# Convolution layers: output projection per third of the tokens, LayerNorm of the later thirds beside it

## The chip, the cores and the metric

The kernel runs on one core of a Trainium2 chip. The metric is the device time of one execution in microseconds. The core has five engines that run their own instruction queues in order: TensorE (PE, matrix multiply), VectorE (DVE), ScalarE (ACT), GpSimd (POOL) and SyncE (SP, which here only issues DMAs). Instructions of different engines wait for each other by semaphores.

## The reference, cut to what matters

A trunk of four layers works on 128 context tokens and 1024 latent tokens of width 1024. Layers 0 and 3 are widened Conformer convolution modules, layer 1 is neighbourhood attention, layer 2 is a state-space mixer. The change concerns the convolution layers:

```python
def conformer_conv_mixer(h, w_in, b_in, w_dw, b_dw, ln_w, ln_b, w_out, b_out):
    v, g, z = jnp.split(h @ w_in + b_in, 3, axis=-1)
    u = v * jax.nn.sigmoid(g)
    u = depthwise_conv(u, w_dw, b_dw)              # 31 taps along the tokens
    u = jax.nn.silu(layer_norm(u, ln_w, ln_b))     # mean and variance over the 1024 channels
    return (u * jax.nn.silu(z)) @ w_out + b_out

# each layer
h, gate = modulated_norm(x, cond, ada_w, ada_b, norm_w)   # RMSNorm(x) * (1 + scale) + shift
x = x + gate * mixer(h)
```

After the last layer a final RMSNorm follows. All is float32.

## The kernel before, in words

Channels lie on the 128 partitions, in eight tiles (KT = 8, index m or k); the 1152 tokens are the free axis, in three thirds of 384 (b = 0, 1, 2; the first holds the context and 256 latent tokens). A product in float32 is made as three products of rounded halves: activations are kept as hh + hl (or gh + gl), weights as wh + wl. A *unit* (`unit`, L471 to L473) is one weight tile of 1024 x 128 times one third: 8 x 3 = 24 matmuls into one PSUM bank.

Weights stream in a fixed order (`weight_specs`): SP loads a raw tile of 512 KB (three buffers), ACT casts it to wh (L432), and one engine named by `w_eng` subtracts to give wl (L433): POOL in the convolution layers, POOL and DVE by turns in part of layer 2. There are two buffers of wh and wl. `ahead` prepares the next one when one is taken.

The order of work is written out by hand with generators. After each unit `tick` (L480 on) pops four depthwise steps, advances the first generator in `gens` three times and runs deferred pieces. A planner then orders the instructions of each engine at build time by a simulated time line, so an instruction can stand earlier or later in its queue than its place in the text.

A convolution layer (`conv_layer`) goes over the channel tiles: the g and v units of tile m, their product u, then the depthwise convolution of that tile as steps: 21 taps on DVE (L773, L775, the sum lies in PSUM as ca) and 10 taps as a scale on ACT (L767) and a sum on POOL (L768), and an addition of both (L784) into c. Tiles of z, the third part of w_in, are put in between as `TAIL` lists them: z tile 5 and 6 come after the last v tile, z tile 7 in the tail. z goes to DRAM and is read back in pieces (zk).

The last channel tile's convolution is split by thirds. Then comes the tail. `conv_norm` of a third has these steps: one for the channel sums by matmul with ones (L648) and the mean (L716); eight that subtract the mean (L720, by turns DVE and POOL), square (ACT, L722) and add up the squares by matmul (L723); the row of variances turned into columns by tiny matmuls (L314), 1/sigma by Newton steps on DVE (L323 to L331), spread over the partitions by a diagonal (dg, L340) and a matmul (rs_ps, L344), four steps later; then eight steps that scale (L731, DVE), silu (L733, ACT), times z (L734, DVE), cast to gh (L735, ACT) and subtract to gl (L736, POOL).

Before the change the tail runs the first third's LayerNorm with four remaining convolution steps beside each of its steps, then all remaining convolution steps of both other thirds, then the rest of the first LayerNorm with the second's first nine steps beside it and z tile 7 between. The pools are closed and others opened, and the output projection (`out_proj`) begins: first a group of the thirds 0 and 1, in which each weight tile serves two units (the first two tiles are taken together), then a group of third 2. The second LayerNorm's rest and the third LayerNorm are generators that advance three steps a unit. Each unit of the projection (`out_unit`) adds the bias on ACT (L557), evicts on DVE (L566), squares on ACT and sums the squares on POOL (L296); in layer 3 it also turns the result (L1517, L1519). After a group the next layer's norm of those thirds follows.

At the start (`start`), layer 0's modulation is computed, and the input norms of the thirds 0 and 1 are written out in front of the first unit; that of third 2 is a generator.

Of the kernel before, what the change touches and what calls it, by code (L numbers as in the profile page):

```python
# [19 lines left out]
P = 128  # L20
# [19 lines left out]
TAIL0 = ([(), (), (0,), (1,), (2,), (3,), (4,), (5, 6)], (7,), 0, 10)  # L40
TAIL3 = ([(), (), (0,), (1,), (2,), (3,), (4,), (5, 6)], (7,), 1, 10)
# [33 lines left out]
REST = 4  # L75
# [5 lines left out]
VAR_MM = 2  # L81
# [93 lines left out]
class Kern:  # L175
    def __init__(self, ctx, tc, A, O, depth):
        self.tc, self.nc, self.A, self.O = tc, tc.nc, A, O
        nc = self.nc
        self.const = ctx.enter_context(tc.tile_pool(name="const", bufs=1))
        self.blkp = ctx.enter_context(tc.tile_pool(name="blk", bufs=9))  # L180
        self.wraw = ctx.enter_context(tc.tile_pool(name="wraw", bufs=3))
        self.wsp = ctx.enter_context(tc.tile_pool(name="wsp", bufs=2))
        self.work = ctx.enter_context(tc.tile_pool(name="work", bufs=2))
        self.dram = ctx.enter_context(tc.tile_pool(name="dram", bufs=1, space=DRAM))
        self.mmp = ctx.enter_context(tc.tile_pool(name="mm", bufs=3, space=PSUM))
        self.xs = [A["x"]] + [self.dram.tile([P, KT, T], F32, name=f"xs{i}") for i in range(1, DEPTH)]
        self.pend, self.steps, self.trickle, self.gens, self.slow = [], [], [], [], []
        self.raws, self.split, self.wi = {}, {}, 0
        self.w_eng = nc.gpsimd
        self.h = [None] * NB  # L190
        self.ada_end = lambda: None
        self.depth = depth
        self.specs = self.weight_specs()
# [113 lines left out]
    def rstd_row(self, row, n, eps):  # L307

        nc = self.nc
        ps = self.mm("st_ps")  # L310
        s = self.work.tile([P, BW], F32, name="row", tag="dg", bufs=1)
        nc.scalar.copy(out=s[0:1, :], in_=row[0:1, :])
        for j in range(3):
            nc.tensor.matmul(ps[:, j:j + 1], lhsT=s[0:1, j * P:(j + 1) * P], rhs=self.ones[0:1, 0:1], start=True,  # L314
                             stop=True)
        return (yield from self.spread(self.rsqrt(ps[:, 0:3], n, eps)))
# [17 lines left out]
    def spread(self, y, times=1.0):  # L334

        nc = self.nc
        for _ in range(LAG):
            yield
# [32 lines left out]
    def weight_specs(self):  # L371
# [5 lines left out]
        for l in range(self.depth):  # L377
# [29 lines left out]
            if kind != 2:  # L407
                out += [(w[m], P) for g in range(2) for m in range(KT)]
# [15 lines left out]
    def wsplit(self, i):  # L424
        if i < len(self.specs) and i not in self.split:
# [7 lines left out]
            self.w_eng.tensor_tensor(out=wl[:, :, :width], in0=s, in1=wh[:, :, :width].bitcast(F32),  # L433
# [46 lines left out]
    def tick(self):  # L480
# [4 lines left out]
        for _ in range(GENS_A_UNIT):  # L485
            self.advance()
# [89 lines left out]
    def out_proj(self, l, g, bias=None, order=None):  # L576
        nc = self.nc
        with self.tc.tile_pool(name="xm", bufs=2, reuse_waits="tile") as pool:
            self.out_begin(l, bias, pool)
            for grp in ((0, 1), (2,)):  # L580
                x0, x1 = (grp[0] * BW, (grp[-1] + 1) * BW) if order is None else (0, T)
                for ms in [(0, 1)] + [(m,) for m in range(2, KT)]:
                    w, xm = {}, {}
                    for m in ms:
                        w[m] = self.wtake()
                        xm[m] = pool.tile([P, x1 - x0], F32, name="xm", tag="xm", bufs=2)
# [17 lines left out]
    def conv_layer(self, l, j, order):  # L604
        nc, tc, h = self.nc, self.tc, self.h
        with tc.tile_pool(name="cp", bufs=1, space=PSUM, reuse_waits="tile") as cp, ExitStack() as stack:
            cw = stack.enter_context(tc.tile_pool(name="cw", bufs=2, reuse_waits="tile"))
            close = stack.close
# [78 lines left out]
            self.lz = cw  # L687
            rest = run(chain(*rest))
            lns[0] = also(lns[0], rest, REST)
            z, nz = chain(*[z_tile(m) for m in TAIL[l][1]]), NB * len(TAIL[l][1])  # L690
            interleave(part(z, TAIL[l][2]), TAIL[l][2], part(lns[0], 9), 9)
            for _ in rest:
                pass
            lns[0] = also(lns[0], part(lns[1], 9))
            interleave(part(lns[0], TAIL[l][3]), TAIL[l][3], z, nz - TAIL[l][2])
            self.flush()
            close()
            with tc.tile_pool(name="lz", bufs=3, reuse_waits="tile") as self.lz:
                for _ in lns[0]:
                    pass  # L700
                self.gens += lns[1:]
                self.out_proj(l, g, bias=("conv_b_out", j * KT), order=order)

    def conv_norm(self, cp, b, j, c, s1, sums, zd, g):

        nc = self.nc
        if b == VAR_MM:
            self.var = cp.tile([P, 3 * 512], F32, name="var", tag="ca", bufs=1)
# [9 lines left out]
        var = self.var[:, 512 * b:512 * b + BW] if b >= VAR_MM else self.mm("var")[:, :BW]  # L718
        for k in range(KT):
# [3 lines left out]
            nc.tensor.matmul(var, lhsT=self.ones, rhs=sq, start=(k == 0), stop=(k == KT - 1))  # L723
            yield
        r = yield from self.rstd_row(var, D, LN_EPS)
        gh, gl = self.blk(f"gh{b}", F32R), self.blk(f"gl{b}", F32R)
        for k in range(KT):
            z = self.lz.tile([P, BW], F32, name="zk", tag="zk", bufs=3)
# [7 lines left out]
            nc.gpsimd.tensor_tensor(out=gl[:, k, :], in0=ck, in1=gh[:, k, :].bitcast(F32), op=ALU.subtract)  # L736
# [802 lines left out]
    def start(self, pool):  # L1539
# [31 lines left out]
        for k in range(KT):  # L1571
# [15 lines left out]
        steps(1, 1 + LAG + 9)  # L1587
# [95 lines left out]
```

## Time and profile before

| | |
|---|---|
| time, median of 3 runs | 2935.44 us (2934.78 to 2937.71) |
| the profiled execution | 2928.56 us, its span 2926.8 us |
| PE busy | 2775.3 us (95%) |
| PE weight loads busy | 2522.4 us (86%) |
| DVE busy | 1976.1 us (68%) |
| ACT busy | 1415.6 us (48%) |
| POOL busy | 1262.1 us (43%) |

The shares are means over the whole span. The two tails of the convolution layers are from about 389 to 580 us and from about 2730 to 2914 us of the span, and what matters in them is read stretch by stretch. Busy time includes time in which an instruction has begun and is held up.

### The profile page before, as it was taken

Reading aid. Unit: us, or ns where it says so; the run is one execution under the profiler, and the core shown is the slowest. Engines: PE = TensorE matmul, PEld = TensorE weight load, DVE = VectorE, ACT = ScalarE, POOL = GpSimd, SP = SyncE. Lnnn points to the kernel's source line nnn. Section 1 sums busy time; section 2 is a strip of 40 time slices with the busy share of each in tenths; the row PEclk is TensorE's granted clock in tenths of the full one; section 3 lists DMA queues with packets and bytes.
Section 4 is the critical chain, followed back from the end, with each engine's and each line's share of the span. In section 5 each row is a group of like instructions: output and inputs, shape, how many; then the busy total and the mean of one; then the engine's idle time right before and its main releaser. Section 6 shows DMA issues by size and latency. Waiting matters only on the chain. (4 is left out here: it accounts for less than half of the span.)

```text
span 2926.8 us, 46350 instructions
## 1 busy us (share of the span) xinstructions
PE 2775.3 (95%) x17561; PEld 2522.4 (86%) x17561; DVE 1976.1 (68%) x3283; ACT 1415.6 (48%) x2764; POOL 1262.1 (43%) x764
## 2 busy tenths in 40 slices
PE   5999998999999999999999999999999999999888
PEld 4999977989999998888999998887778889999678
DVE  5899886553444444536787677866885565999973
ACT  4455455443333333444443336865663444555553
POOL 4688766601011101245113442312433346888765
PEclk9999999999999999999999999999999999999989
DMA  5232324632222323336235559977896752111134
GB/s 223 68 121 98 103 78 150 210 118 79 82 83 89 92 81 102 121 102 208 81 89 160 162 166 314 342 219 229 271 322 227 253 176 85 55 65 53 62 122 142
DMA packets 231551, 424.48 MB, mean 145 GB/s; under 512 B 19552, under 2 KB 149408, under 8 KB 231328
## 3 DMA queue, kind: packets, MB, share of 16 engines
q1 hardware_dynamic: 229280, 417.50, 44.1%
q10 hardware_dynamic: 2048, 4.02, 0.4%
q8 instruction: 139, 2.28, 0.3%
q14 instruction: 84, 0.69, 0.1%
HBM read 331.83 MB, written 79.66 MB: 141 GB/s over the span
## 5 line engine op out<-in xcount | busy, mean ns | idle before, releaser
L433 POOL TENSOR_TENSOR wl<-raw,wh 128x1024 fp32r<-128x1024 f32 x169 | 408.3, 2417 | 951.4 <-ACT wh L432 909.5
L775 DVE SCALAR_TENSOR_TENSOR ca<-u,vec,ca 128x1167 f32<-128x1167 f32 (+4 forms) x420 | 481.4, 1146 | 11.3
L768 POOL TENSOR_TENSOR pa<-pa,pt 128x1167 f32<-128x1167 f32 (+4 forms) x189 | 399.6, 2117 | 78.4 <-ACT pa L763 36.4
L432 ACT CAST wh<-raw 128x1024 fp32r<-128x1024 f32 (+1 forms) x239 | 249.3, 1043 | 351.0 <-PE op L472 84.9
L471 PE MATMUL in_ps<-hh,wh 128*128 128x384 f32 x768 | 268.4, 352 | 4.2 <-DVE nt L866 3.0
L472 PE MATMUL in_ps<-hl,wh 128*128 128x384 f32 x768 | 262.4, 342 | 0.7 <-DVE hl L364 0.7
L473 PE MATMUL in_ps<-hh,wl 128*128 128x384 f32 x768 | 261.9, 341 | 0.0
L767 ACT ACTIVATE pt<-u,vec 128x1167 f32<-128x1167 f32 (+4 forms) x189 | 193.9, 1039 | 128.3 <-POOL pa L768 127.2
L471 PE MATMUL op<-gh,wh 128*128 128x384 f32 x576 | 202.0, 353 | 18.2 <-ACT gh L735 12.0
L1410 ACT ACTIVATE rw<-rw,nal 128x128 f32<-128x128 f32 x576 | 175.8, 389 | 76.0 <-DMA rw<-ssd_rows 75.9
L473 PE MATMUL op<-gh,wl 128*128 128x384 f32 x576 | 199.9, 348 | 10.1 <-POOL wl L433 10.1
L1289 DVE SCALAR_TENSOR_TENSOR sca<-ub,vec,sca 128x1155 f32<-128x1155 f32 x144 | 205.0, 1424 | 3.5
L471 PE MATMUL x_ps<-hh,wh 128*128 128x384 f32 x576 | 203.9, 354 | 1.3 <-ACT ub L1240 0.7
L472 PE MATMUL op<-gl,wh 128*128 128x384 f32 x576 | 202.0, 351 | 0.5 <-POOL gl L736 0.5
L473 PE MATMUL x_ps<-hh,wl 128*128 128x384 f32 x576 | 196.5, 342 | 0.0
L472 PE MATMUL x_ps<-hl,wh 128*128 128x384 f32 x576 | 196.5, 341 | 0.0
L471 PEld LDWEIGHTS in_ps<-hh,wh 128*128 128x128 f32 x768 | 145.3, 189 | 13.8 <-issue 7.3
L296 POOL TENSOR_TENSOR ssq<-ssq,sq 128x384 f32<-128x384 f32 x105 | 111.6, 1064 | 86.5 <-ACT sq L295 85.3
L472 PEld LDWEIGHTS in_ps<-hl,wh 128*128 128x128 f32 x768 | 145.6, 190 | 3.2 <-DVE hl L364 1.5
L473 PEld LDWEIGHTS in_ps<-hh,wl 128*128 128x128 f32 x768 | 145.5, 189 | 3.1 <-issue 2.4
L471 PE MATMUL op<-sgh,wh 128*128 128x384 f32 x384 | 135.6, 353 | 5.1 <-DVE xm L566 2.6
L473 PE MATMUL op<-sgh,wl 128*128 128x384 f32 x384 | 134.4, 350 | 4.8 <-POOL wl L433 4.3
(280 smaller groups left out, 7552.4 us busy)
## 6 DMA issues: line engine op xcount, KB each, us to landing
raw<-in_ada_w SPq DMA_DIRECT2D x96, 512.0 KB, 4.5
rw<-ssd_rows SPq DMA_DIRECT2D x72, 512.0 KB, 5.9
raw<-in_ssd_w_in SPq DMA_DIRECT2D x62, 512.0 KB, 4.4
raw<-in_conv_w_in SPq DMA_DIRECT2D x48, 512.0 KB, 3.5
raw<-in_ssd_w_out SPq DMA_DIRECT2D x48, 512.0 KB, 4.6
raw<-in_conv_w_out SPq DMA_DIRECT2D x32, 512.0 KB, 3.7
raw<-in_na_w_in SPq DMA_DIRECT2D x32, 512.0 KB, 3.6
ssd_xtok<-xtk SPq DMA_DIRECT2D x20, 576.0 KB, 3.6
```

Source lines behind the costliest of these rows:

```text
L296: nc.gpsimd.tensor_tensor(out=acc, in0=acc, in1=sq, op=ALU.add)
L432: nc.scalar.copy(out=wh[:, :, :width], in_=s)
L433: self.w_eng.tensor_tensor(out=wl[:, :, :width], in0=s, in1=wh[:, :, :width].bitcast(F32), op=ALU.subtract)
L471: nc.tensor.matmul(out, lhsT=wh[:, k, :width], rhs=hh[:, k, :], start=f, stop=False)
L472: nc.tensor.matmul(out, lhsT=wh[:, k, :width], rhs=hl[:, k, :], start=False, stop=False)
L473: nc.tensor.matmul(out, lhsT=wl[:, k, :width], rhs=hh[:, k, :], start=False, stop=l)
L767: nc.scalar.activation(out=pt, in_=u_t, func=AF.Copy, scale=wt(t))
L768: nc.gpsimd.tensor_tensor(out=p, in0=p, in1=pt, op=ALU.add)
L775: nc.vector.scalar_tensor_tensor(out=c, in0=u_t, scalar=wt(t), in1=c, op0=ALU.mult, op1=ALU.add)
L1289: nc.vector.scalar_tensor_tensor(out=ca, in0=u[:, t:t + SCLEN], scalar=wt(t), in1=ca, op0=ALU.mult, op1=ALU.add)
L1410: nc.scalar.activation(out=e, in_=e, func=AF.Identity, bias=self.nal[:, c, d, 8 * g + q:8 * g + q + 1])
```

## The change

- `TAIL`: z tile 6 joins z tile 7 in the tail, in both layers.
- The remaining convolution steps of the second and the third third are kept apart. The first LayerNorm has two steps of the second third beside each of its first nine steps, with z tile 6; then z tile 7 beside the 1/sigma chain; then one such step beside each of its last steps. All that remains (the second third's last steps, the second LayerNorm, the last third's convolution one step beside each of its steps, the third LayerNorm) becomes one generator, advanced five steps a unit in the projection.
- `out_proj` in these layers goes through three groups of one third, so that each weight tile is loaded, cast and split once for each third: 24 instead of 16. Its pool is the convolution's own, which stays open; xm has the buffers of sg and zt, zk is three parts of an old u buffer.
- In that projection every third weight split is DVE's.
- `conv_norm`: the variance's bank is one of the two of the sums (for the last third that of ca); from the second third on, the variance matmul comes one step after its square, and the 1/sigma matmuls three and twelve steps later; every second gl is DVE's.
- `start`: the spread of the first norm comes one pair of modulation tiles later; the second third's norm is a generator.

```diff
-TAIL0 = ([(), (), (0,), (1,), (2,), (3,), (4,), (5, 6)], (7,), 0, 10)
-TAIL3 = ([(), (), (0,), (1,), (2,), (3,), (4,), (5, 6)], (7,), 1, 10)
+TAIL0 = [(), (), (0,), (1,), (2,), (3,), (4,), (5,)], (6, 7)
+TAIL3 = TAIL0
-REST = 4
+REST = 2, 1
+LAG_TAIL = 12
+RATE_TAIL = 5
...
-    def rstd_row(self, row, n, eps):
+    def rstd_row(self, row, n, eps, lag):
...
+        for _ in range(lag // 4 - 1):
+            yield
...
-        for _ in range(LAG):
+        for _ in range(lag):
             yield
...
+            eng = self.w_eng[i % len(self.w_eng)] if isinstance(self.w_eng, list) else self.w_eng
...
-        for _ in range(GENS_A_UNIT):
+        for _ in range(self.rate):
             self.advance()
...
+            grps = ((0,), (1,), (2,)) if pool else ((0, 1), (2,))
...
-                for ms in [(0, 1)] + [(m,) for m in range(2, KT)]:
+                for ms in [(0, 1)] + [(m,) for m in range(2, KT)] if len(grps) == 2 else [(m,) for m in range(KT)]:
...
-            self.lz = cw
-            rest = run(chain(*rest))
-            lns[0] = also(lns[0], rest, REST)
-            z, nz = chain(*[z_tile(m) for m in TAIL[l][1]]), NB * len(TAIL[l][1])
-            interleave(part(z, TAIL[l][2]), TAIL[l][2], part(lns[0], 9), 9)
-            for _ in rest:
+            self.zk = [up[KT % 3][:, i * BW:(i + 1) * BW] for i in range(3)]
+            rest = [run(r) for r in rest]
+            ln0 = also(lns[0], rest[0], REST[0])
+            z = chain(*[z_tile(m) for m in TAIL[l][1]])
+            interleave(part(ln0, 9), 9, part(z, 3), 3)
+            interleave(part(lns[0], 1 + LAG), 1 + LAG, z, 3)
+            for _ in also(lns[0], rest[0], REST[1]):
                 pass
-            lns[0] = also(lns[0], part(lns[1], 9))
-            interleave(part(lns[0], TAIL[l][3]), TAIL[l][3], z, nz - TAIL[l][2])
             self.flush()
-            close()
-            with tc.tile_pool(name="lz", bufs=3, reuse_waits="tile") as self.lz:
-                for _ in lns[0]:
-                    pass
-                self.gens += lns[1:]
-                self.out_proj(l, g, bias=("conv_b_out", j * KT), order=order)
+            self.gens += [chain(rest[0], also(lns[1], rest[1], 1), rest[1], lns[2])]
+            self.rate, self.w_eng = RATE_TAIL, [nc.gpsimd, nc.vector, nc.gpsimd]
+            self.out_proj(l, g, bias=("conv_b_out", j * KT), order=order, pool=cw)
+            self.rate, self.w_eng = GENS_A_UNIT, nc.gpsimd
...
-        var = self.var[:, 512 * b:512 * b + BW] if b >= VAR_MM else self.mm("var")[:, :BW]
+        shape, tag, bufs = ([P, 512], "s1", 2) if b < 2 else ([P, 3 * 512], "ca", 1)
+        var, todo = cp.tile(shape, F32, name="var", tag=tag, bufs=bufs)[:, :BW], []
...
-            nc.tensor.matmul(var, lhsT=self.ones, rhs=sq, start=(k == 0), stop=(k == KT - 1))
+            todo.append((k, sq))
+            if b == 0 or len(todo) == 2:
+                i, q = todo.pop(0)
+                nc.tensor.matmul(var, lhsT=self.ones, rhs=q, start=(i == 0), stop=(i == KT - 1))
             yield
-        r = yield from self.rstd_row(var, D, LN_EPS)
+        for i, q in todo:
+            nc.tensor.matmul(var, lhsT=self.ones, rhs=q, start=False, stop=True)
+        r = yield from self.rstd_row(var, D, LN_EPS, LAG_TAIL if b else LAG)
...
-            z = self.lz.tile([P, BW], F32, name="zk", tag="zk", bufs=3)
+            z = self.zk[k % 3]
...
-            nc.gpsimd.tensor_tensor(out=gl[:, k, :], in0=ck, in1=gh[:, k, :].bitcast(F32), op=ALU.subtract)
+            (nc.gpsimd if k % 2 else nc.vector).tensor_tensor(out=gl[:, k, :], in0=ck, in1=gh[:, k, :].bitcast(F32),
+                                                              op=ALU.subtract)
...
             if k == NORM_0:
-                steps(0, 1 + LAG + k)
+                steps(0, 1)
+            elif k == NORM_0 + 1:
+                steps(0, LAG + k)
...
-        steps(1, 1 + LAG + 9)
+        self.gens.append(norms[1])
```

## Rows read from the trace of the kernel before

**Rows 1.** Busy time by stretch, layer 0's tail: stretch, length, busy (instructions), clock, DMA.

```profile
398.00:441.00 43.00, 35.53 (x133) 25.09 (x134) 40.79 (x67) 22.06 (x46) 23.22 (x19) 0.88 0.17 59
441.00:480.00 39.00, 28.36 (x120) 23.82 (x120) 29.88 (x44) 21.05 (x44) 26.19 (x23) 0.87 0.49 153
...
497.00:560.00 63.00, 61.41 (x354) 60.48 (x353) 32.68 (x58) 33.92 (x63) 43.73 (x29) 1.00 0.62 210
```

**Rows 2.** The same, tail of layer 3 (PE, PEld, DVE, ACT, POOL).

```profile
2736.00:2775.00 39.00, 29.75 (x104) 19.11 (x104) 38.34 (x64) 23.66 (x46) 27.21 (x24) 0.96 0.03 8
2775.00:2801.00 26.00, 15.47 (x62) 13.46 (x62) 23.20 (x44) 12.34 (x26) 14.16 (x14) 0.71 0.43 143
...
2834.00:2914.00 80.00, 78.86 (x474) 77.35 (x473) 38.58 (x81) 38.64 (x67) 52.29 (x35) 1.00 0.41 135
```

**Rows 3.** Waits, 395 to 581 us: who waited for whom, total, times, longest.

```profile
PE rs_ps L344 <- DVE dg L340: 8.1, 3, 5.0
PE op L471 <- ACT gh L735: 8.1, 2, 6.5
...
PE op L473 <- POOL wl L433: 5.5, 4, 2.1
```

**Rows 4.** DVE's groups, 395 to 581: count, busy us, mean ns, idle before.

```profile
L734 DVE TENSOR_TENSOR c<-c,zk 128x384 f32<-128x384 f32 x24 | 22.2, 961 | 5.0 <-DMA zk<-zd 2.8 <-ACT gh L735 1.1 <-ACT sq L722 1.0
L775 DVE SCALAR_TENSOR_TENSOR ca<-u,vec,ca 128x384 f32<-128x384 f32 x32 | 19.8, 618 | 0.5
L731 DVE SCALAR_TENSOR_TENSOR c<-c,vec,rstd 128x384 f32<-128x384 f32 x24 | 17.6, 801 | 2.3 <-ACT rstd L346 2.3
L566 DVE SCALAR_TENSOR_TENSOR xr<-op,mod,nt 128x384 f32<-128x384 f32 (+2 forms) x32 | 15.5, 510 | 42.7 <-PE op L473 42.7
...
L720 DVE TENSOR_TENSOR c<-c,mu 128x384 f32<-128x384 f32 x12 | 11.2, 986 | 0.0
```

**Rows 5.** Timeline of DVE and POOL at the ends of stretches: start us, us, instructions merged.

```profile
388.24 0.62 DVE L784 TENSOR_TENSOR c<-ca,pa 128x128 f32<-128x128 f32 x2
...
450.10 1.02 DVE L734 TENSOR_TENSOR c<-c,zk 128x384 f32<-128x384 f32 x2
...
452.09 8.06 DVE L731 SCALAR_TENSOR_TENSOR c<-c,vec,rstd 128x384 f32<-128x384 f32 x8 [0.97 <-ACT rstd L346]
...
453.53 5.14 POOL L720 TENSOR_TENSOR c<-c,mu 128x384 f32<-128x384 f32 x4
...
2729.80 0.62 DVE L784 TENSOR_TENSOR c<-ca,pa 128x128 f32<-128x128 f32 x2 [0.17 <-POOL pa L768]
...
2785.98 1.36 DVE L734 TENSOR_TENSOR c<-c,zk 128x384 f32<-128x384 f32 x1
```

**Rows 6.** Timeline of PE inside a full unit.

```profile
369.68 0.33 PE L471 MATMUL z_ps<-hh,wh 128*128 128x384 f32 x1
...
370.20 0.33 PE L471 MATMUL z_ps<-hh,wh 128*128 128x384 f32 x1
```

**Rows 7.** PE's groups, 390 to 700: count, busy us, mean ns, idle.

```profile
L723 PE MATMUL var<-sq,ones 128*128 128x384 f32 x48 | 19.8, 520 | 0.0
```

**Rows 8.** Single lines over the whole span: duration ns shortest/median/longest.

```profile
L433 POOL TENSOR_TENSOR wl<-raw,wh x169: 1282/2397/3579, 35.2 to 2906.0; 128x1024 fp32r<-128x1024 f32 x168, 128x512 fp32r<-128x512 f32 x1
...
L433 DVE TENSOR_TENSOR wl<-raw,wh x70: 1200/1225/2083, 1756.4 to 2347.2; 128x1024 fp32r<-128x1024 f32 x70
...
L734 DVE TENSOR_TENSOR c<-c,zk x48: 543/1000/2470, 436.3 to 2848.8; 128x384 f32<-128x384 f32 x48
...
L736 POOL TENSOR_TENSOR gl<-c,gh x48: 995/1236/1341, 441.3 to 2854.0; 128x384 fp32r<-128x384 f32 x48
```

**Rows 9.** Waits of PE, 2350 to 2430, end of layer 2's projection.

```profile
PE op L473 <- POOL wl L433: 4.3, 3, 2.1
```

**Rows 10.** Timeline of PE, last matmul of layer 0's projection.

```profile
579.41 0.34 PE L473 MATMUL op<-gh,wl 128*128 128x384 f32 x1
```

**Rows 11.** Timeline of PE in front of the first unit.

```profile
62.72 1.62 PE L344 MATMUL rs_ps<-dg,ones 128*128 128x384 f32 x2 [7.81 <-DVE dg L340]
```

More of the change, by code (lines that the diff above doesn't have):

```diff
@@ L80 @@
 VEC0 = sum(n for _, n in VECS[:4])
-VAR_MM = 2
 NA_FIRST = (0, 1), (2,), (3,)
@@ L189, in __init__ @@
         self.w_eng = nc.gpsimd
+        self.rate = GENS_A_UNIT
         self.h = [None] * NB
@@ L315, in rstd_row @@
                              stop=True)
-        return (yield from self.spread(self.rsqrt(ps[:, 0:3], n, eps)))
+        return (yield from self.spread(self.rsqrt(ps[:, 0:3], n, eps), lag=lag))
     def rsqrt(self, x, n, eps):
@@ L332, in rsqrt, with spread @@
         return y
-    def spread(self, y, times=1.0):
+    def spread(self, y, times=1.0, lag=LAG):
         nc = self.nc
-        for _ in range(LAG):
+        for _ in range(lag):
             yield
@@ L407, in weight_specs @@
             if kind != 2:
-                out += [(w[m], P) for g in range(2) for m in range(KT)]
+                out += [(w[m], P) for g in range(NB if kind == 0 else 2) for m in range(KT)]
         return out
@@ L574, in out_unit, with out_proj @@
             nc.sync.dma_start(out=self.xs[l + 1][:, :, b * BW:(b + 1) * BW], in_=self.xb[b])
-    def out_proj(self, l, g, bias=None, order=None):
+    def out_proj(self, l, g, bias=None, order=None, pool=None):
         nc = self.nc
-        with self.tc.tile_pool(name="xm", bufs=2, reuse_waits="tile") as pool:
+        with ExitStack() as stack:
+            grps = ((0,), (1,), (2,)) if pool else ((0, 1), (2,))
+            pool = pool or stack.enter_context(self.tc.tile_pool(name="xm", bufs=2, reuse_waits="tile"))
             self.out_begin(l, bias, pool)
-            for grp in ((0, 1), (2,)):
+            for grp in grps:
                 x0, x1 = (grp[0] * BW, (grp[-1] + 1) * BW) if order is None else (0, T)
-                for ms in [(0, 1)] + [(m,) for m in range(2, KT)]:
+                for ms in [(0, 1)] + [(m,) for m in range(2, KT)] if len(grps) == 2 else [(m,) for m in range(KT)]:
                     w, xm = {}, {}
@@ L605, in conv_layer @@
         nc, tc, h = self.nc, self.tc, self.h
-        with tc.tile_pool(name="cp", bufs=1, space=PSUM, reuse_waits="tile") as cp, ExitStack() as stack:
-            cw = stack.enter_context(tc.tile_pool(name="cw", bufs=2, reuse_waits="tile"))
-            close = stack.close
+        with tc.tile_pool(name="cp", bufs=1, space=PSUM, reuse_waits="tile") as cp, \
+                tc.tile_pool(name="cw", bufs=2, reuse_waits="tile") as cw:
             up = [cw.tile([P, ULEN], F32, name=f"u{i}", bufs=1) for i in range(3)]
```

7 lines of the change are left out of this document (3 added, 4 removed).

## The prediction

> **What bounds the kernel now.** I read first the busy share of each engine in stretches of the two convolution tails, then the waits there, then VectorE's groups, then the timeline at the ends of the stretches. In the first tail PE is busy 35.5 of 43 us, then 28.4 of 39, then 61.4 of 63; in the last layer's it is 29.8 of 39 and 15.5 of 26, then 78.9 of 80 [rows 1, 2]. So PE loses time from the end of the depthwise convolution until two thirds of the tokens have passed their LayerNorm, and is full from there. In those stretches DVE is busy 40.8 of 43 and 38.3 of 39 us. What PE waits for are products of LayerNorm: the normalised gh, 8.1 us, and the row of 1/sigma (dg), 8.1 us; late weights (wl) cost 5.5 us [rows 3]. The granted clock is 0.88 and 0.87 in the two loose stretches of layer 0 and 0.71 in the loosest of layer 3, against 1.00 where PE is full [rows 1, 2]: a pause also makes the matmuls behind it slower.
>
> The timeline says why DVE is late. The first third of the last convolution tile is done at 388.9 and at 2730.4; the last multiplies by z that this third's gh waits for start at 450.1 and 2786.0 [rows 5]. These 62 and 56 us hold all taps of both other thirds (32 of L775, 19.8 us [rows 4]) and part of the second LayerNorm, and then the second third is wanted after two units of projection.
>
> **The change, part by part.** The sum is made in the profiled run's own clock: span 2926.8, the run 2928.56. The median of the runs shown is 2935.44, so 6.9 us are added at the end.
>
> Unit prices. Three matmuls of a unit start every 0.52 us [rows 6], so a unit of 24 takes 4.17 us. With what lies between, I take 4.35 in layer 0 and 4.7 in layer 3, where each unit also turns its result (17 units in the 80 us full stretch, 474 records [rows 2]). A pass of statistics (eight matmuls of the variance, or seven of the sum) is a third of the 19.8 us of row L723, less the overlap of its pairs: 5.8 us [rows 7]. DVE prices are means of the same stretch [rows 4]: subtract mean 1.0 (four a third, POOL has the other four), scale 0.73 to 0.80, times z 0.96, a tap 0.62, eviction 15.5 us for 20 units = 0.78. The 1/sigma chain counts 5.0, the longest wait of PE for it [rows 3].
>
> *First LayerNorm.* Of the second third's 32 convolution steps two now go with each of nine LayerNorm steps and one with each of eight, 26 in all, some 18 of them DVE's taps; the last third's stay behind the first gh. DVE: entry 2 (estimate), subtract 4, taps 18 x 0.62 = 11, chain 5, scale 8 x 0.8 = 6.4, times z 7.7, and the four gl that move here from POOL, 4 x 0.96 = 3.8 by the nearest two-input row: 40 us. The first gh is whole at 429 instead of 451 and at 2770.5 instead of 2787. PE meanwhile has two z tiles, 25 us, of which the moved one fills the time in which DVE still runs taps; it cost 12.5 us of PE before and costs the same now. If it were placed too late it would stand after gh, at worst 12.5 us a layer.
>
> *Second LayerNorm beside eight units.* DVE between first and second gh: three taps 2, all 21 taps of the last third 13, subtract 4, chain 5, scale 6.4, times z 7.7, gl 3.8, evictions 6.2, and one weight split in three. That split on DVE has rows from the SSD layer: 1.20 to 2.08 us, median 1.23 [rows 8]; 2.7 of them at 1.4 make 3.7. Sum 52 us; in layer 3 also eight copies of turned output (0.5 each, estimate by L566), 56. PE has after its first unit (paced by gh, done 2 us after it) seven more and a variance pass: 7 x 4.35 + 5.8 = 36 in layer 0, 7 x 4.7 + 5.8 = 39 in layer 3. So PE would wait 52 - 2 - 36 = 14 and 56 - 2 - 39 = 15 us. With the shortest times seen in place of means (times z 0.543 [rows 8]; 0.55 for subtract and gl, an estimate by it) the DVE sum falls by 4 + 2 + 2 + 1 and the wait to 5. I take 8 us: POOL loses a half of its gl here but keeps 2.39 us for each of two splits in three, so I stand between the ends.
>
> *Third LayerNorm beside eight units.* DVE 4 + 5 + 6.4 + 7.7 + 3.8 + 6.2 + 3.7 = 37; PE 36, and the sums of the last third, 5.8, that no longer come early since their bank is now shared with the variance. 42 against 37: no wait in layer 0, 45 against 41 in layer 3.
>
> *The end of each tail.* From the first finished unit (431, 2772.5) PE has 23 units and three passes of statistics: 23 x 4.35 + 17.4 = 117.5 and 23 x 4.7 + 17.4 = 125.5. Without waiting it is done at 548.5 and 2898, with 8 us at 556.5 and 2906. Now the projection ends at 579.7 [rows 10] and at 2914 [rows 2]; the 12.8 us from there to the span's end stay. Gains: 23 and 8 us.
>
> *Eight more weight tiles a layer.* A tile for each unit instead of one for two. A weight is cast on ACT and split on POOL, the split alone 2.39 us [rows 8] against 4.35 of PE, in two buffers. The last 80 us of the SSD layer's projection already run so, one weight a unit, with the next layer's norm beside them: 4.3 us of waits for wl [rows 9], in 80 / 4.7 = 17 units 0.3 us each, and that is inside the 4.35. The loads: 1.1 MB a unit at most, as in the full stretch 497 to 560, whose DMA share is 0.62 [rows 1]; I cost them at nothing. If that cover is gone, the cast waits behind SP's queue, where the z slices now wait for one of three pieces of an old buffer, as they do now for one of three tiles.
>
> *Lag of the matmuls, rate 5, the variance's bank.* Each takes a wait of PE's queue away where DVE is late; what is then late is gh itself, counted above. Zero by themselves.
>
> *The start.* The first unit stands behind a 1/sigma matmul of the second third, which waits 7.8 us for DVE until 62.7 [rows 11]. With the change that norm comes behind the first unit. Its own DVE chain ends no earlier, and the third unit hangs on it, so at most the 7.8 us come back, and if its matmul slides behind a whole unit 4.2 are lost. I take -3.
>
> Sum: -23 - 8 - 3 = -34, 2894.6 for a run like the profiled one, 2901 beside the median.
>
> **A rule weighed.** Where POOL is busy, times z takes 1.0 us in the median and up to 2.47, where 0.543 is its shortest, and POOL's gl 1.24 against 0.995 [rows 8]. In one stretch four subtracts on POOL (5.14 us) ran beside eight scales on DVE (8.06 us) [rows 5]: the 2.9 us that DVE had alone hold some five scales at 0.55 to 0.6 (estimate by times z's 0.543), so the 5.14 us hold four POOL pieces and three scales, whose short times add up to 4.0 + 1.8 = 5.8. They overlap by little. The Trainium skill, SBUF — State Buffer, section Who interferes with whom, says that a DVE instruction with two SBUF inputs and a GpSimd one that reads SBUF exclude each other, the second blocked until the first ends. The trace nearly agrees (5.14 for 5.8). By that rule the gl and splits moved to DVE stand in one line with POOL's work; what that gives is the second rival.
>
> **The rivals.**
> 1. *The waits vanish* (DVE's short times hold; chance 0.15): 548.5 and 2898, start -6: -31 - 16 - 6 = -53, 2882. For it: POOL has less to do. Against: 38.3 of 39 us DVE [rows 2].
> 2. *POOL and DVE take turns* (0.18). Beside the first eight units POOL has 5.3 splits x 2.39, 8 square sums, 8 LayerNorm pieces and 11 tap sums at 1.0 each (estimate by gl's 0.995), 40 us; DVE's two-input work is 17 us by shortest times. 57 in line; the third LayerNorm 46. PE then waits 20 us in layer 0 and 15 in layer 3: -11 - 2 - 3 = -16, 2919. For it: the 2.47 us in [rows 8] and the pair in [rows 5]. Against: the 52 us of DVE above already hold the slowed means, and only what exceeds them is new.
> 3. *The weight feed decides, slower* (0.16). Place: 32 units in two layers have a LayerNorm beside them and a weight of their own. ACT's cast stands in order behind silu and casts of gh, and holds them up when it waits for a weight buffer; the split stands behind LayerNorm on POOL. Price: the longest wait for wl is 2.1 us [rows 3, 9]. From 34 / 32 = 1.1 us a unit the gain is gone; at 2 us the time is 2935 - 34 + 64 = 2965. Against: 0.3 us a unit in [rows 9].
> 4. *The order stays* (0.06): instructions are issued in the order a planner finds at build time; if it hoists the same work as now, 2935.
>
> **How the numbers follow.** Forecast 0.45, own range 2890 to 2912. The range 2871 to 2932 takes in rivals 1, 2 and the middle of 4; left out are rival 3 beyond its point, and little below. 0.2% (5.9 us) is what a measurement can tell here. Faster: 0.45 + 0.15 + 0.18 + 0.01 = 0.79; same: 0.05 of rival 4 and 0.02 of 3 = 0.07; slower 0.14.
>
> **What would show it.** The last multiply for the first third's gh near 429 and 2770; one wait of PE for gh of 5 to 15 us after eight units and none after sixteen; projection over near 556 and 2906; L433 wl waits under 10 us a layer. Wrong: wl or wh as PE's largest waits (rival 3), times z well over 1.0 us in the mean (rival 2), or a first gh later than 440, which would say the planner put other work in front.

## The result and the profile after

| | before | after |
|---|---|---|
| median of 4 runs | 2936.24 us (2934.78 to 2937.71) | 2962.68 us (2959.22 to 2964.99) |
| span of the profiled execution | 2926.8 us | 2962.0 us |
| layer 0: last v matmul, first and last matmul of the projection | 366.1, 440.9, 579.7 | 363.3, 438.6, 598.9 |
| layer 3: the same | 2704.4, 2775.2, 2914.0 | 2721.5, 2797.6, 2948.7 |

The ratio is 1.0097, with a 95% interval of 1.0080 to 1.0114: 26 us slower, where 34 us faster was forecast. From the last v matmul to the end of the projection layer 0 now takes 235.6 us (213.6 before), layer 3 227.2 us (209.6). The profiled run of the kernel before is 7.7 us under its median and the changed one 1.1 us over: that is why the spans are 35 us apart and the medians 26.

Busy time of the changed kernel in the stretches of [rows 1] and [rows 2]; columns as there (PE, PEld, DVE, ACT, POOL, granted clock, DMA):

```profile
398.00:441.00 43.00, 30.35 (x125) 22.41 (x124) 41.42 (x72) 22.29 (x44) 20.77 (x18) 0.84 0.41 138
441.00:480.00 39.00, 37.63 (x192) 34.28 (x191) 14.08 (x31) 19.08 (x37) 19.24 (x13) 0.96 0.55 178
497.00:560.00 63.00, 52.17 (x263) 47.00 (x261) 47.95 (x82) 34.53 (x64) 30.72 (x20) 0.92 0.64 219
...
2834.00:2914.00 80.00, 64.42 (x324) 56.91 (x323) 63.88 (x98) 42.70 (x76) 48.02 (x29) 0.89 0.47 149
```

The first unit comes only 2.3 us earlier. The next stretch, loose before, is nearly full (37.6 of 39 us). But the stretches that were full are loose now: 52.2 of 63 us where it was 61.4, and 64.4 of 80 where it was 78.9, with DVE busier by 15 and 25 us (in layer 3 the work arrives some 20 us later, so that the stretch still holds a part of the LayerNorms). With the pauses the granted clock there falls from 1.00 to 0.92 and 0.89.

Waits of PE in the changed kernel, 395 to 600 us (total, times, longest), beside [rows 3]:

```profile
PE rs_ps L348 <- DVE dg L344: 18.1, 3, 9.1
PE var L729 <- ACT sq L725: 11.8, 3, 10.8
PE op L476 <- ACT gh L743: 6.3, 1, 6.3
PE op L478 <- POOL wl L438: 3.2, 2, 2.0
PE op L477 <- DVE gl L744: 2.5, 1, 2.5
```

Weights are hardly waited for (3.2 us). Two of the waits for dg, 8.1 and 9.1 us, stand in front of the next layer's norms, at 549 and 569 us; a wait of 10.8 us for the second LayerNorm's squares stands in front of the first unit. DVE at the second dg, and POOL beside it, from the changed kernel's timelines (start, us):

```profile
557.38 2.28 DVE L368 SCALAR_TENSOR_TENSOR hl<-nt,mod,hh 128x128 fp32r<-128x128 f32 x1
...
566.41 0.16 DVE L333 SCALAR_TENSOR_TENSOR nr_z<-nr_y,nr_a 128x3 f32<-128x3 f32 x1
566.61 0.96 DVE L334 TENSOR_TENSOR nr_z<-nr_z,nr_y 128x3 f32<-128x3 f32 x1
567.60 0.16 DVE L335 SCALAR_TENSOR_TENSOR nr_y<-nr_z,nr_y 128x3 f32<-128x3 f32 x1
```

```profile
557.12 2.40 POOL L438 TENSOR_TENSOR wl<-raw,wh 128x1024 fp32r<-128x1024 f32 x1 [7.79 <-ACT wh L436]
566.56 0.99 POOL L298 TENSOR_TENSOR ssq<-ssq,sq 128x384 f32<-128x384 f32 x1 [7.04 <-ACT sq L297]
```

This is the reading to learn. An instruction of 0.16 us on three columns takes 0.96 us because it began 0.05 us after a POOL instruction of 0.99 us, and ends with it. A subtraction on 128 columns takes 2.28 us beside a weight split of 2.40 us. DVE counts as busy all that time, and the wait of PE is written against dg, not against POOL. The whole stretch, 395 to 600 us of the changed kernel, says the same: the scale of 384 columns (L739) takes 0.61 us in the mean of the 13 that no POOL instruction overlaps and 1.45 us in the 11 that one does; times z (L742) takes 0.55 and 1.07; a convolution tap (L784), whose sum lies in PSUM, takes 0.62 both ways.

### The profile page after: what moved, and what is told of

It is laid out like the page before. It is cut to its first block, busy times and chain, and to the rows that moved or that the text cites. A ratio compares the mean times of both kernels' runs of the same rounds, so it can differ in the third digit from the quotient of the medians.

```text
span 2962.0 us, 46434 instructions
## 1 busy us (share of the span) xinstructions
PE 2790.2 (94%) x17561; PEld 2534.5 (86%) x17561; DVE 2007.2 (68%) x3323; ACT 1436.4 (48%) x2780; POOL 1244.7 (42%) x740
## 3 DMA queue, kind: packets, MB, share of 16 engines
q8 instruction: 139, 2.28, 0.3%
## 5 line engine op out<-in xcount | busy, mean ns | idle before, releaser
L784 DVE SCALAR_TENSOR_TENSOR ca<-u,vec,ca 128x1167 f32<-128x1167 f32 (+4 forms) x420 | 481.5, 1146 | 11.3
L436 ACT CAST wh<-raw 128x1024 fp32r<-128x1024 f32 (+1 forms) x255 | 266.4, 1045 | 375.7 <-PE op L477 94.2
L298 POOL TENSOR_TENSOR ssq<-ssq,sq 128x384 f32<-128x384 f32 x105 | 118.5, 1129 | 83.7 <-ACT sq L297 82.2
L438 DVE TENSOR_TENSOR wl<-raw,wh 128x1024 fp32r<-128x1024 f32 x86 | 112.0, 1302 | 46.2 <-ACT wh L436 45.5
```

Of the source, the lines that this page charges most:

```text
L298: nc.gpsimd.tensor_tensor(out=acc, in0=acc, in1=sq, op=ALU.add)
L436: nc.scalar.copy(out=wh[:, :, :width], in_=s)
L784: nc.vector.scalar_tensor_tensor(out=c, in0=u_t, scalar=wt(t), in1=c, op0=ALU.mult, op1=ALU.add)
```

## The experiments

Ratios are against the kernel before, run on the same chip beside each group of runs. Its median there is 2936.4 us for a to d, 2932.9 for e to h, 2933.5 for i, j, k and m, and 2932.5 for n, o and p. Two versions are compared by their medians; by the spread of the runs such a difference is good to 4 to 7 us (9 for h), and between groups it also holds up to 4 us of the chips. All edits but the last lie in the two convolution layers; m also changes a lag in the norms behind them.

**Undoing orders in the changed kernel.** Four runs: the rate back to three (a), a shorter lag (b), the first LayerNorm in front of the last taps on DVE (c), all three (d).

```diff
-            self.gens += [chain(rest[0], also(lns[1], rest[1], 1), rest[1], lns[2])]
+            self.gens += [chain(rest[0], also(lns[1], rest[1], 1), rest[1], lns[2], self.slow_down())]   # a: rate = 3
...
-LAG_TAIL = 12
+LAG_TAIL = 4                                           # b
...
+            rest[1] = self.behind(rest[1], self.last_mul)   # c: each step issued behind the first LayerNorm's last L742
```

> The rate of side work goes back from five steps a unit to three once the convolution's LayerNorms are through, so that the next layer's norms run at the old spacing. Theory 2 (at rate five the multiply that spreads a norm's 1/std stands one unit behind its row): the two PE waits for dg in layer 0 (8.1 and 9.1 us in the changed kernel) go to under 1 us each, layer 3 has no such wait, and the time falls by 13 to 17 us, to about 2947. Theories 1 and 3 (the LayerNorms' chains) and the rivals (24 weights to feed, POOL and DVE on one port) are not touched by it: by them alone it stays within 3 us of 2963.

> The lag between the later LayerNorms' statistics and the matmul that spreads 1/std is cut from 12 steps to 4. Theory 1 (the second LayerNorm is late because its short chain stands at fixed places among PE's units, with DVE idle): 1/std of layer 0 is there some 5 to 7 us earlier, the wait for the second gh (6.3 and 2.5 us for gl in layer 0, 8.5 us in layer 3) goes to under 3 us, the time falls by 8 to 15 us, to about 2951. Rival 1 (DVE's load or POOL and DVE in turns makes the second LayerNorm late): the wait stays above 5 us and the time within 3 us of 2963. Rival 2 (the lag was needed): a PE wait of 3 to 6 us for dg appears at the shortened place and eats the gain.

> DVE's queue gets the last third's taps of the last convolution tile behind the last product of the first LayerNorm, by an order written into the kernel, not left to the planner. Theory 3 (the planner's order puts 20 taps of 620 ns in front of the first LayerNorm's multiplies): the first gh is whole near 429 instead of 441 in layer 0, the first projection unit starts 9 to 12 us earlier in both layers, the time falls by 18 to 24 us, to about 2942. If the second LayerNorm or the weight feed sets the end whatever comes first, the first unit is earlier but the projection ends where it did, the wait for the second gh grows by as much, and the time stays within 5 us of 2963.

> The three edits together (rate back to three for the next layer's norms, lag 4, last taps behind the first LayerNorm's products). If the three theories hold and add up: 15 + 12 + 22 us off, about 2914, 22 us below the kernel before. If the second LayerNorm's place bounds what an earlier first gh can give: about 2935. If the weight feed of 24 weights or the port decides: above 2950.

Measured: a 2956.7 (1.0077, 1.0058 to 1.0095), b 2963.3 (1.0097, 1.0078 to 1.0116), c 2959.0 (1.0081, 1.0063 to 1.0099), d 2946.5 us (1.0043, 1.0025 to 1.0062). So a is worth 6 us, b nothing, c 4 (a and c are hardly beyond the spread), all three 16: a third of the 49 us expected, and no mending. In a, the dg wait fell to 9.0 us, but a wait of 8.2 us for an eviction came in front of the next layer. In b the wait for the second gh went (6.3 us), and the longest dg wait grew from 9.1 to 11.9. In c the first unit started at 438.9, where 429 was expected. PE's timeline of d:

```profile
420.42 0.81 PE L655 MATMUL s<-c,ones 128*128 128x384 f32 x2
431.59 1.65 PE L741 MATMUL var<-sq,ones 128*128 128x384 f32 x2 [10.36 <-ACT sq L737]
433.03 5.86 PE L655 MATMUL s<-c,ones 128*128 128x384 f32 x14
438.72 0.81 PE L741 MATMUL var<-sq,ones 128*128 128x384 f32 x2
439.07 0.81 PE L476 MATMUL op<-gh,wh 128*128 128x384 f32 x2
```

The planner puts two variance matmuls of the second LayerNorm ahead of the first unit, and PE waits there for squares that DVE's and ACT's queues hold behind the first LayerNorm. That is not all: gh itself is whole no earlier than in the changed kernel (440.4 us there, 440.4 in c, 440.9 in d). In c DVE has dg done at 415.2, but PE, which has z to do, comes to its matmul only at 419.4, and then rstd stands in ACT's queue behind a wait for xm and the cast of a weight:

```profile
419.92 0.80 ACT L562 ACTIVATE nt<-xm,gb 128x128 f32<-128x128 f32 x2 [2.05 <-DMA xm<-in_x]
420.63 1.03 ACT L436 CAST wh<-raw 128x1024 fp32r<-128x1024 f32 x1
...
422.04 0.47 ACT L350 ACTIVATE rstd<-rs_ps 128x384 f32<-128x384 f32 x1
```

So the scale of the first LayerNorm begins at 422.8 us in c and at 423.9 in the changed kernel, though 19 taps of the last third have left its way. A chain that is put right in one queue waits in the next.

**One part alone, on the kernel before.** f: the projection by thirds with 24 weight tiles. g: z tiles 6 and 7 in the tail.

```diff
-            for grp in ((0, 1), (2,)):
+            for grp in ((0,), (1,), (2,)) if bias else ((0, 1), (2,)):                        # f
-                for ms in [(0, 1)] + [(m,) for m in range(2, KT)]:
+                for ms in [(m,) for m in range(KT)] if bias else [(0, 1)] + [(m,) for m in range(2, KT)]:
...
-TAIL0 = ([(), (), (0,), (1,), (2,), (3,), (4,), (5, 6)], (7,), 0, 10)
+TAIL0 = ([(), (), (0,), (1,), (2,), (3,), (4,), (5,)], (6, 7), 3, 10)                         # g
```

> The kernel before with one part of the change alone: the convolution's output projection goes third by third with 24 weight tiles; the LayerNorms, the z tiles, the rate and all of POOL's work stay as they were. If the projection per third is sound by itself: the 6.5 us that the first unit of the second third waits in the kernel before goes, in both layers, and the time is 2 to 13 us below the kernel before, about 2928. If feeding 24 weights instead of 16 is what costs (8 more splits of 1.05 us on ACT and 2.4 us on POOL a layer): PE waits for wl by over 10 us a layer and the time is 15 to 30 us above, about 2958.

> The kernel before with another part alone: z tile 6 comes out of the loop, and tiles 6 and 7 stand beside the first LayerNorm, three of their units with its statistics, three with the rest. If the two z tiles are useful cover: the 5.0 us that PE waits for the first 1/std goes and the time falls by 4 to 10 us, about 2929. If the first LayerNorm's chain on DVE, ACT and POOL sets the start of the projection, three more units beside it only fill PE time: within 4 us of the kernel before.

f: 2961.5 us (1.0091, 1.0074 to 1.0108). The projection by thirds alone costs 28.6 us over the 2932.9 of before, as much as the whole change. Waits of PE in f, 441 to 620 us, and in the kernel before, 441 to 620:

```profile
PE rs_ps L344 <- DVE dg L340: 13.4, 3, 9.6
PE op L473 <- POOL wl L433: 12.3, 8, 2.5
PE op L471 <- ACT wh L432: 11.8, 4, 5.3
```

```profile
PE op L473 <- POOL wl L433: 5.5, 4, 2.1
PE rs_ps L344 <- DVE dg L340: 3.1, 2, 2.7
...
PE op L471 <- ACT wh L432: 1.5, 2, 0.9
```

Here the late weights are seen as such (24.1 us for wl and wh, 7.0 before), and again dg. The wait of 6.5 us for the second third's gh is gone, as the change meant it. g: 2943.2 us (1.0031, 1.0017 to 1.0044), 10 us slower, which neither expectation had. Its first unit starts 73.8 us after the last v matmul (74.8 before): the two z tiles cover nothing that sets that time. Where the 10 us are lost its profiled run does not show: its two tails are 210.9 and 213.4 us long, beside 213.6 and 209.6. Of the 15 us between the two spans 5 stand before the tail of layer 0 and 8 between the tails, where the edit changes nothing. That stays open.

**POOL out of the projection, and wholly in it.** On d: gl and wl all on DVE (e), all on POOL (h).

```diff
-            (nc.gpsimd if k % 2 else nc.vector).tensor_tensor(out=gl[:, k, :], in0=ck, in1=gh[:, k, :].bitcast(F32),
-                                                              op=ALU.subtract)
+            nc.vector.tensor_tensor(out=gl[:, k, :], in0=ck, in1=gh[:, k, :].bitcast(F32), op=ALU.subtract)   # h: nc.gpsimd
...
-            self.rate, self.w_eng = RATE_TAIL, [nc.gpsimd, nc.vector, nc.gpsimd]
+            self.rate, self.w_eng = RATE_TAIL, nc.vector          # h: nc.gpsimd
```

> The version with all three edits, and in the projection all gl and wl subtractions on DVE: POOL keeps the sums of squares and half of the c - mu. If turns with POOL are what makes DVE's short chains long (steps of 0.16 us take 0.9 to 2.3 us while POOL works), the waits for dg in layer 0 go from 15.8 to under 8 us and the time falls by 5 to 15 us under that version's 2946. If DVE's own load is (12 gl of 0.55 and 16 wl of 1.22 us more, 26 us a layer), the waits for xr and dg grow and the time rises by 8 us or more.

> The version with all three edits, and in the projection all gl and wl subtractions on POOL, as before the change: 12 gl and 8 wl a layer leave DVE, some 17 us of its time, and lengthen POOL's by 31. If DVE's load makes the chains late, dg and xr waits fall and the time goes 5 to 12 us under 2946. If turns with POOL do, the steps of the short chains get longer, and the time rises by 5 us or more; if the weight's low part gets late, PE waits for wl by over 5 us a layer.

e: 2932.1 us (0.9989, 0.9973 to 1.0005), 14 us under d. h: 2963.5 (1.0104, 1.0079 to 1.0128), 17 us over it. DVE's load is not the bound: it got 12 gl and 16 wl a layer more in e, and the time fell. But the sign that the turns lengthen the 1/sigma chain on PE's path did not come: PE waits 14.0 us for dg in layer 0 in e, 15.8 in d, where under 8 was expected, though the chain's steps got shorter (L333 403 ns in the mean in d, 202 in e). Two things leave with POOL at once, its turns with DVE and its own longer subtractions (wl 2.4 us against 1.25, gl 1.2 against 0.6), and no run parts them.

**The same edit on the kernel before, with and without thirds.** i: the kernel before with gl on DVE, and w_eng on DVE from the start of the projection to its end. k: f with gl and wl on DVE. j: f without the eight extra splits a layer. m: e with two more orders.

```diff
-                        w[m] = self.wtake()
+                        w[m] = last if bias and grp == (1,) else self.wtake()      # j, o: with 16 weights in weight_specs
+                        last = w[m]
...
+            also(self.behind(lns[1], self.last_mul), rest[1], 1)                   # m, and LAG 12 in the next layer's norms
```

> The kernel before, with only the engine changed: the gl subtractions and, in the convolution layers' projection, the wl subtractions go from POOL to DVE. If POOL's turns with DVE are a cost in any arrangement, the time falls by 6 to 15 us under the kernel before, to about 2925. If they cost only where 24 weights are split, it stays within 5 us of the kernel before; if DVE's load decides, it rises.

> The kernel before with the projection third by third, as in the earlier run of that part alone (2961), but the second third's eight units all use the last weight tile of the first third: the eight extra loads and splits a layer are left out, and with them the right weights of that third. All units, LayerNorms and evictions stay. If the eight extra splits (8 casts on ACT, 8 subtractions of 2.4 us on POOL a layer) are what costs, the time falls from 2961 to 2935 or less. If the order by thirds costs by itself (one unit a weight, the norms at other places), it stays above 2950.

> The kernel before with the projection third by third and 24 weights, and gl and wl subtractions on DVE. All 24 casts on ACT and the 24 loads stay. If it is the extra splits on POOL that cost the 28 us, most comes back: 2930 to 2942. If it is the casts on ACT, the loads, or the order by thirds, it stays above 2950.

> The version with three edits and gl and wl on DVE (2932), and two more: the second LayerNorm's steps stand behind the first one's last product, so that PE does not stop for its squares ahead of the first unit; and the next layer's norms have 12 steps between their sums and the matmul that spreads 1/std, not 4. If the two remaining waits of PE in layer 0 (10.3 us for the squares, 14.0 us for dg) are on the path, both go under 3 us and the time falls by 10 to 20 us, to about 2917, below both kernels. If other chains stand right behind them, it falls by under 5 us.

i: 2917.3 us (0.9940, 0.9924 to 0.9956). j: 2945.9 (1.0045, 1.0031 to 1.0058). k: 2927.1 (0.9981, 0.9969 to 0.9992). m: 2928.6 (0.9976, 0.9965 to 0.9987). So the subtractions on POOL cost 16 us in the kernel before too, and 34 us where there are 24 weight tiles (k against f). The extra tiles cost 15.6 us with POOL (j against f). What k lacks of f's waits is in layer 0 above all the late weights, 24.1 us in f; in k, 441 to 620 us:

```profile
PE op L471 <- ACT wh L432: 1.3, 2, 1.1
...
PE op L473 <- DVE wl L433: 1.0, 2, 0.7
```

In layer 3 it is PE's wait for evicted tiles that it is to turn: 14.7 us in f, 0.4 in k. So with 24 tiles late weights from POOL are a part of the price, beside the lengthened chains. j stays 13 us above the kernel before, between its two expectations, so there the order by thirds costs something by itself as well. DVE's groups in f, 395 to 600 us (count, busy, mean ns, idle), and then in k, in which DVE does more:

```profile
L329 DVE SCALAR_TENSOR_TENSOR nr_z<-nr_y,nr_a 128x3 f32<-128x3 f32 x15 | 8.6, 572 | 0.4
L331 DVE SCALAR_TENSOR_TENSOR nr_y<-nr_z,nr_y 128x3 f32<-128x3 f32 x15 | 6.5, 434 | 0.4
...
L326 DVE TENSOR_SCALAR nr_y<-nr_y 128x3 int32<-128x3 int32 x5 | 5.1, 1012 | 0.1
```

```profile
L329 DVE SCALAR_TENSOR_TENSOR nr_z<-nr_y,nr_a 128x3 f32<-128x3 f32 x18 | 4.7, 261 | 0.4
L331 DVE SCALAR_TENSOR_TENSOR nr_y<-nr_z,nr_y 128x3 f32<-128x3 f32 x18 | 4.1, 227 | 0.5
...
L326 DVE TENSOR_SCALAR nr_y<-nr_y 128x3 int32<-128x3 int32 x6 | 1.5, 251 | 0.1
```

The short chain's steps take about half the time or less. In m the first unit starts at 429.4, and it no longer waits for squares but for gh itself, which is whole at 436.3, 4 us before the changed kernel's and 7 after the forecast's:

```profile
429.43 1.01 PE L477 MATMUL op<-gh,wh 128*128 128x384 f32 x2 [10.24 <-ACT gh L756]
```

Its layer 0 is through at 569.6 us, with no wait for the second gh. Yet in the median it is within 4 us of e, and 11 us slower than i, which leaves the old order alone.

**What was open: the engine alone on the changed kernel (n), thirds without extra splits on DVE (o), the start on top of i (p).**

```diff
-                steps(0, 1 + LAG + k)
+                steps(0, 1)
+            elif k == NORM_0 + 1:
+                steps(0, LAG + k)                 # p: i with the change's start
...
-        steps(1, 1 + LAG + 9)
+        self.gens.append(norms[1])
```

> The changed kernel with one edit: in the projection all gl and wl subtractions on DVE. If POOL's turns with DVE are the larger part of the loss, by themselves and not only together with the other three edits, the time falls from 2963 by 10 to 18 us, to about 2949. If they only show once the chains are put right, it falls by under 5 us.

> The kernel before with the projection third by third, gl and wl subtractions on DVE, and the second third's units using the first third's last weight tile, so that the eight extra loads and splits a layer, and with them the right weights of that third, are left out. With the splits it took 2927, with two groups and 16 weights 2917. If the 10 us between are the extra splits (8 casts of 1.05 us on ACT, 8 subtractions of 1.22 us on DVE a layer): 2916 to 2920. If they are the order by thirds (the next layer's first norm beside the third LayerNorm on DVE): it stays at 2925 to 2929.

> The kernel before with gl and wl subtractions of the projection on DVE and the change's new start (the first layer's norms begin one tile later and the second norm is left to the units). The start alone reached the first layer's last v unit 2.7 us earlier in the changed kernel: 2914 to 2915 if it adds up with the 2917 of the engine's change. If the lower granted clock that goes with it in the first 200 us eats it: 2917 or more.

n: 2939.7 us (1.0026, 1.0012 to 1.0040), 23 us under the changed kernel by this edit alone, or 19 if each is counted from the kernel before on its own chip (10 to 18 expected). In the profiled runs 17 of 29 us lie in the two tails and 12 between them, in layers whose code is the same and which take 2110 to 2133 us in the profiled runs; so the traces place the gain only in part. DVE's groups in the changed kernel and in n, 395 to 600 us:

```profile
L739 DVE SCALAR_TENSOR_TENSOR c<-c,vec,rstd 128x384 f32<-128x384 f32 x24 | 22.2, 991 | 0.4 <-ACT rstd L350 0.3
...
L742 DVE TENSOR_TENSOR c<-c,u 128x384 f32<-128x384 f32 x24 | 18.1, 788 | 7.2 <-DMA u<-zd 7.2
...
L571 DVE SCALAR_TENSOR_TENSOR xr<-op,mod,nt 128x384 f32<-128x384 f32 (+2 forms) x32 | 15.7, 512 | 30.4 <-PE op L478 26.0 <-ACT sq L725 4.2 <-ACT nt L562 0.2
...
L744 DVE TENSOR_TENSOR gl<-c,gh 128x384 fp32r<-128x384 f32 x12 | 10.4, 872 | 1.9 <-ACT gh L743 1.6
L438 DVE TENSOR_TENSOR wl<-raw,wh 128x1024 fp32r<-128x1024 f32 x8 | 9.8, 1231 | 1.0 <-ACT wh L436 0.6 <-issue 0.4
```

```profile
L438 DVE TENSOR_TENSOR wl<-raw,wh 128x1024 fp32r<-128x1024 f32 x24 | 30.3, 1265 | 2.3 <-ACT wh L436 2.3
...
L739 DVE SCALAR_TENSOR_TENSOR c<-c,vec,rstd 128x384 f32<-128x384 f32 x24 | 17.9, 812 | 0.4 <-ACT rstd L350 0.3
L571 DVE SCALAR_TENSOR_TENSOR xr<-op,mod,nt 128x384 f32<-128x384 f32 (+2 forms) x32 | 15.6, 512 | 24.0 <-PE op L478 20.7 <-ACT nt L562 3.3
L744 DVE TENSOR_TENSOR gl<-c,gh 128x384 fp32r<-128x384 f32 x24 | 13.6, 595 | 0.4 <-ACT gh L743 0.3
L742 DVE TENSOR_TENSOR c<-c,u 128x384 f32<-128x384 f32 x24 | 13.4, 583 | 6.7 <-DMA u<-zd 6.6
```

DVE does 28 more instructions in these lines (16 wl, 12 gl) and the LayerNorm's lines that read two operands from SBUF get shorter: scale 991 to 812 ns, times z 788 to 583, gl 872 to 595. (wl, which met little of POOL before, does not: 1231 and 1265.) The eviction L571, which has one operand in PSUM, stays at 512. The Trainium skill, SBUF — State Buffer, section Who interferes with whom, has a DVE instruction with two SBUF inputs and a GpSimd one that reads SBUF exclude each other, and leaves out one with at most a single SBUF input outside the two-port modes; these rows agree with both halves.

o: 2909.6 us (0.9921, 0.9900 to 0.9943), below both its expectations. The extra tiles cost 17.5 us with DVE (against k), and thirds without them are 7.7 us faster than two groups (against i). p: 2909.7 us (0.9920, 0.9894 to 0.9946): the new start is worth 7.6 us (against i), where 2 to 3 were expected. p, unlike o, leaves nothing out, and is the fastest version of all that do not: 23 us below the kernel before, 53 below the changed one. Its full stretch, which was 52.2 of 63 in the changed kernel:

```profile
497.00:560.00 63.00, 62.35 (x361) 61.49 (x360) 44.41 (x93) 33.47 (x62) 18.62 (x14) 1.00 0.68 238
```

The medians as one table (us):

| | gl, wl on POOL | gl, wl on DVE |
|---|---|---|
| two groups, 16 weight tiles | 2932.9 (before) | 2917.3 (i); 2909.7 with the new start (p) |
| thirds, 24 weight tiles | 2961.5 (f) | 2927.1 (k) |
| thirds, 16 tiles (part left out) | 2945.9 (j) | 2909.6 (o) |

## Why the prediction was wrong

**The steps that failed** are two terms of the sum.

The first is "Eight more weight tiles a layer": "I cost them at nothing". They cost 15.6 us for sixteen tiles (f less j), 17.5 with DVE splitting (k less o), some 1.0 us a tile and a quarter of the 61 us between forecast and median. The evidence was the end of the SSD layer's projection, with 0.3 us of wait for wl a unit [rows 9], a stretch with no convolution LayerNorm beside it. Much of the price is not in that wait: between j and f, 395 to 600 us, PE's waits for wl grow from 5.7 to 10.5 us and those for dg from 11.9 to 18.9; between o and k those for wl from 0.5 to 1.0 and those for dg from 5.5 to 11.0. In the changed kernel PE waits 3.2 us for wl in layer 0. Under "what would show it" I had written that wl waits below 10 us a layer would speak for me; that mark was blind. Since the price is as high where DVE splits, turns with POOL are not all of it; casts and loads are common to both pairs, and no run has them alone.

The second is "The end of each tail": "Without waiting it is done at 548.5 and 2898, with 8 us at 556.5 and 2906". From the last v matmul that is 190.4 and 201.6 us; measured are 235.6 and 227.2, 45 and 26 us more. Of these, 15 and 12.5 us are there when the first unit is done (443.1 and 2802.1 us): the first gh came late. The other 30 and 13 us lie behind it. In layer 0 PE stands idle 32 us from the first unit on, where the sum had 8; 17.2 of them are waits for the next layer's norms, which the sum did not have, and 8.8 are for the second third's gh and gl. Moving the last subtractions off POOL alone returns 19 to 23 us of the whole (n).

- *Rival 3, the weight feed decides:* its time (2965) came out by luck. It was 64 us for 32 units; measured are 15.6 for sixteen tiles, and the sign, wl or wh as PE's largest waits, did not come in the changed kernel. Late weights do show in f, 24.1 us. Its first reason, that ACT's cast holds up the queue, does not tell the slow version from the fast one: the casts wait 16.2 us for PE in f and 13.9 in k (441 to 620 us).
- *Rival 2, POOL and DVE take turns:* that they take turns shows in DVE's durations, and that subtractions on POOL cost shows in e, h, i, k and n; how much of that is the turns and how much POOL's own longer subtractions is not shown. I priced it at 18 us of lost gain, since "the 52 us of DVE above already hold the slowed means". They held before's meetings with POOL, not those of eight more splits; and I did not see that the kernel before loses 16 us to POOL's subtractions. The mark I gave it, times z well over 1.0 us in the mean, failed: it is 0.79 in the changed kernel (1.03 in f, 0.58 in n).
- *First gh at 429 and 2770.5:* it was whole at 440.4, the last cast of gh in the timeline, and the first unit came at 438.6 and 2797.6. The planner did put the last taps first, which 440 was the mark for. But c and d, with those taps behind, have gh whole at 440.4 and 440.9: the 1/sigma matmul then stood in PE's queue and rstd in ACT's, which the sum of DVE's work did not hold. The second LayerNorm's variance matmuls in PE's queue ("Zero by themselves") held the first unit back too, by little, since gh was whole only after it began. m, with these behind as well and gl, wl on DVE, has gh whole at 436.3.
- *Second LayerNorm beside eight units, wait 8:* measured 6.3 for gh and 2.5 for gl in layer 0, 8.5 in layer 3. The size came out by luck: in 441 to 480 DVE is busy 14.1 of 39 us, so its load was not the reason. The chain was late by its place among the units; with a shorter lag (b) that wait went, and the time stayed. The sum's evictions were also misread: 15.5 us are those of 24 units, 0.65 us each, not of 20, which is 1 us here.
- *Third LayerNorm, no wait:* no wait for gh, as said; but the next layer's norms came in its way on DVE, and PE waited 17.2 us for dg in layer 0. Nothing in my sum had them. With the rate put back (a) 6 us returned.
- *Moved z tile at no cost:* alone on the kernel before, the two z tiles lost 10 us (g).
- *Start −3:* layer 0's last v matmul came 2.8 us earlier, as forecast, but against an early one: it ends at 366.1 to 371.5 in the seven profiled runs with the old start, at 359.4 to 364.9 in the ten with the new. In the time p gains 7.6.

Put together from the medians: thirds +28.6 (f), z tiles +10.3 (g), start -7.6 (p), and the change's own move of half of gl and a third of wl to DVE about -17 (d against h) make +14. The other 12 us of the 26 fall by subtraction to the order, lag and rate of the LayerNorms; undoing three of these took back 16 (d). Each term is good to some 5 us, and the terms act on each other, so this is an account, not a proof: with POOL the order by thirds costs 13 us (j), with DVE it gains 8 (o).

What stays open: how the price of POOL's subtractions divides between its turns with DVE and its own longer times, what in the extra tiles costs as much with DVE as with POOL, where g loses its 10 us, and what of j's 13 us is POOL's queue and what the casts on ACT, for which PE waits 10.1 us in its layer 0.

## What to carry to other kernels

Before adding work to GpSimd beside a VectorE chain, compare the duration of VectorE's shortest instructions with and without a GpSimd instruction under them; if they stretch to its length, the GpSimd work is serial with VectorE, and VectorE may do it sooner itself (here a split in 1.25 us for 2.4), though it looks full. A wait names the last link: a new cost on a shared resource can show in none of the waits that bear its name, so try a suspect by moving it to another engine or leaving it out. A reordering in which a weight tile serves fewer units pays for the extra tiles before it gains anything, here about 1 us a tile.

## What the runs showed of the hardware

I had not expected that moving 28 instructions a layer onto the engine that looked full would make the kernel some 20 us faster (n) and its other lines shorter, nor that one-operand steps on three int32 values (L326) would stretch like the two-operand ones: in f the four that a POOL instruction overlaps take 1.22 us in the mean, the one alone 0.17; the mean is 1012 ns in f and 251 in k, with less on POOL.
